# A 3x3 convolution with 2x2 max-pool: ten row sums that read their odd rows from PSUM, casts moved between engines, and a new program order

## The chip, the core and the metric

The kernel runs on one core of a Trainium2 chip. The time is device microseconds of one execution. Five engines matter: TensorE (PE in the profile; its weight loads are PEld), VectorE (DVE), ScalarE (ACT), GpSimd (POOL) and SyncE (SP, which here only issues transfers). Each engine takes its instructions in order and waits on semaphores that other engines and transfers raise.

## The reference

The input x has 16 images of 64 channels and 64x64 pixels, the weights are 128x64x3x3, all float32. The output is the convolution with padding 1, of which the maximum over every 2x2 window is kept: 16 images of 128 channels and 32x32.

```python
for co in range(c_out):
    for ci in range(c_in):
        for kh in range(k):
            for kw in range(k):
                conv[b, co] += weight[co, ci, kh, kw] * x_pad[b, ci, kh:kh+h, kw:kw+w]
...
output[b, c, i, j] = np.max(conv[b, c, i*2:(i+1)*2, j*2:(j+1)*2])
```

## The kernel before

Two images lie side by side in the 128 partitions, 64 channels each (half 0 and half 1). A pair of images is cut into four quarters of 16 rows, so there are 32 steps; a step makes 8 pooled rows of both images. Every product of a step is three matmuls, one per column of the filter, over 64 partitions and up to 512 columns, and lands in one PSUM bank (8 rows of 64). There are eight banks, held in `acc`; a queue `free` gives them out.

The two rows of a pooling window share work: the sum or difference of input rows meets a sum or difference of filter rows. `TYPES` gives each step one of two forms.

- K steps (11 of them) hold x as bf16 (`kx`), loaded with a cast by GpSimd's transfers (`LK`) or cast on chip. PA1 and PA2 build bank `ta`, PB1 and PB2 bank `tb`, and PR adds a product of the row sum `ks` (step KS, a VectorE add).
- W steps (21) hold x as float32 (`wx`, three buffers, loaded by SP: `L`, or `LB`, which also waits for the last VectorE instruction that was marked with `on_vector`). They need three bf16 tiles: `we` (even rows less odd rows, step E), `wd` (each row less the one above, step D, always GpSimd) and `ws` (even rows plus odd rows, step WS, always VectorE). P2 and P0 build `ta`; P3 and P1 build `tb`.

Behind the products: SE copies `ta` to `tb` on ScalarE (W steps, between P2 and P0/P3); EV copies `ta` to SBUF on ScalarE; MX takes the maximum of `tb` and that copy on VectorE, in place; then the shared product (PR or P1) is added; OD copies the odd columns to SBUF on ScalarE; CM takes the maximum of even and odd columns on VectorE; a store follows the second half's CM, on SP. Each of these exists for half 0 and half 1, so `MX.31.1` is step 31, half 1.

`DIFF_ON_VECTOR` names the steps whose E is on VectorE, all others are on GpSimd. `SUM_BY_REDUCTION` names the steps whose WS is a `tensor_reduce` over pairs of rows (one input of 1024 elements) in place of a `tensor_tensor` with two inputs of 512. GpSimd's tensor instructions wait for the last marked VectorE instruction that stands ahead of them in the program (`on_gpsimd`); the `tensor_reduce` isn't marked, the `tensor_tensor` is.

The head: eight matmuls of ones first; the weights arrive as `wraw`, are cast (g0, g1, g2), combined (D0, D2, GS, GM, GP), turned on TensorE (T...), copied out of PSUM (V...). The first K step is cast on chip from `kfirst`, in four pieces (XEa, XEb even rows, XOa, XOb odd rows), the second from `ksecond` (X1, X2). The first K step's products are cut in halves (F.k.part), the first W step's too (G.k.part), with E and D in halves Ea, Eb, Da, Db and the copies SEa, SEb.

The order of everything is written out by hand in `ORDER`, one long list of step names; each engine runs its own steps in that order. Products go through `lanes`: one is issued when a product of the other half stands by, and the six matmuls alternate between the two. Such a couple is called a pair below; there are 132, apart from the halves of F and G.

Of the kernel before, what the change touches and what calls it, by code (L numbers as in the profile page):

```python
# [11 lines left out]
def kernel(  # L12
# [37 lines left out]
    d_pool = ctx.enter_context(tc.tile_pool(name="d_pool", bufs=5))  # L50
    e_pool = ctx.enter_context(tc.tile_pool(name="e_pool", bufs=5))
    ws_pool = ctx.enter_context(tc.tile_pool(name="ws_pool", bufs=5))
    ks_pool = ctx.enter_context(tc.tile_pool(name="ks_pool", bufs=4))
    ev_pool = ctx.enter_context(tc.tile_pool(name="ev_pool", bufs=7))
    od_pool = ctx.enter_context(tc.tile_pool(name="od_pool", bufs=6))
    o_pool = ctx.enter_context(tc.tile_pool(name="o_pool", bufs=6))
# [125 lines left out]

# [85 lines left out]
    def first_product(k, part):  # L268
        s, q = KSTEPS[0], 0
        m0, first, where, skip = (  # L270
            (D2, 1, ta, None),
            (G0, -1, ta, 0),
            (D0, 0, tb, None),
            (G2, 2, tb, None),
        )[k]
        span = (0, R // 2) if part == 0 else (R // 2, R)
        start = k in (0, 2) and part == 0
# [115 lines left out]
    ev, od, ot, made = {}, {}, {}, {}  # L393
# [39 lines left out]
    def colmax(s, h):  # L433
# [5 lines left out]
        made[s] = made.get(s, 0) + 1  # L439
# [10 lines left out]
    def cast_rows(lo, hi):  # L450
        on_vector(nc.vector.tensor_copy(out=kx[0][:, lo:hi:2, :], in_=kfirst[:, lo:hi:2, :]))  # L451

    def cast_more(first):
# [13 lines left out]
        "GM": lambda: on_vector(nc.vector.tensor_sub(out=slots(GM), in0=gsum, in1=g1)),  # L467
        "GP": lambda: on_vector(nc.vector.tensor_add(out=slots(GP), in0=gsum, in1=g1)),
        "XOa": lambda: cast_rows(1, kmid),
        "XOb": lambda: cast_rows(kmid, khi),  # L470
        "XEa": lambda: cast_rows(0, kmid),
        "XEb": lambda: cast_rows(kmid + 1, khi),
# [11 lines left out]
        "SE": seed, "EV": evac, "MX": rowmax, "OD": odd, "CM": colmax,  # L484
    }
# [4 lines left out]
    for m in PRODUCTS:  # L490
# [8 lines left out]
        EV.2.1 P1.3.1 SE.3.1 EV.2.0 WS.3 MX.1.1 P1.1.0 SE.3.0 P0.3.0 MX.2.0 MX.2.1 EV.3.1 PR.2.0 EV.3.0 D.4  # L499
        MX.3.1 OD.2.0 PA1.5.1 OD.1.0 E.4 PA1.5.0 PA2.5.0 P3.3.0 OD.1.1 OD.2.1 L.12 L.14 PA2.5.1 OD.3.1  # L500
        P2.4.1 CM.1.1 CM.2.0 P2.4.0 CM.1.0 PA1.7.1 D.6 EV.5.0 CM.3.1 CM.2.1 MX.3.0 PA2.7.1 PB1.5.1 SE.4.0
        PA1.7.0 PA2.7.0 EV.5.1 SE.4.1 EV.7.0 PB2.5.1 P0.4.1 P0.4.0 P2.6.1 KS.7 E.6 P3.4.1 WS.4 WS.6 P1.3.0
        EV.4.0 PR.5.1 KS.5 WS.8 EV.7.1 P0.6.1 PB1.5.0 PB1.7.0 PB2.5.0 PB2.7.0 L.16 P1.4.1 EV.4.1 MX.5.1
        P3.4.0 OD.3.0 SE.6.1 MX.5.0 LK.1.0 LK.1.1 CM.3.0 MX.4.1 P3.6.1 OD.5.1 PB1.7.1 MX.7.0 PB2.7.1 PR.5.0
        OD.5.0 P2.6.0 EV.6.1 E.8 PR.7.0 MX.4.0 OD.4.1 OD.7.0 CM.5.1 D.8 P1.4.0 SE.6.0 OD.4.0 CM.5.0 E.9
        MX.6.1 CM.7.0 CM.4.0 P1.6.1 P2.8.0 CM.4.1 D.9 P2.8.1 SE.8.0 P0.6.0 P2.9.1 MX.7.1 P3.6.0 OD.6.1
        EV.6.0 P0.8.0 L.17 P3.8.0 SE.8.1 CM.6.1 PR.7.1 EV.8.0 OD.7.1 P0.8.1 MX.6.0 SE.9.1 E.11 MX.8.0 P1.6.0
        D.11 CM.7.1 P2.9.0 OD.6.0 EV.8.1 CM.6.0 WS.9 P3.8.1 P1.8.0 P0.9.1 PA1.10.1 SE.9.0 P2.11.0 OD.8.0
        L.19 L.20 P3.9.1 PA2.10.1 KS.10 EV.9.1 SE.11.0 P0.9.0 CM.8.0 E.14 P2.11.1 MX.9.1 P3.9.0 MX.8.1
        P0.11.0 EV.9.0 EV.10.1 MX.9.0 P1.9.1 D.14 E.12 P1.8.1 PA1.10.0 P3.11.0 PA2.10.0 SE.11.1 OD.9.1  # L510
        P1.9.0 P2.14.0 WS.11 CM.9.1 P0.11.1 P3.11.1 EV.11.0 EV.11.1 OD.8.1 OD.9.0 EV.10.0 P1.11.0 PA1.13.0
        PA1.13.1 MX.11.0 MX.11.1 PA2.13.1 D.12 L.22 L.23 PA2.13.0 P2.12.0 CM.8.1 CM.9.0 D.16 P1.11.1 EV.13.1
        P2.12.1 OD.11.0 SE.14.0 OD.11.1 PB1.10.1 WS.14 P0.14.0 CM.11.0 PB2.10.1 P3.14.0 CM.11.1 L.24 P0.12.0
        SE.12.1 P0.12.1 SE.12.0 P3.12.1 P3.12.0 EV.14.0 PB1.10.0 P2.14.1 WS.12 PB2.10.0 EV.13.0 MX.10.1
        EV.12.1 MX.14.0 E.16 EV.12.0 MX.12.1 PR.10.1 P1.14.0 MX.12.0 SE.14.1 OD.10.1 P1.12.0 PB1.13.1
        PA1.18.0 KS.15 KS.13 CM.10.1 P0.14.1 MX.10.0 OD.14.0 P3.14.1 CM.14.0 EV.14.1 P1.12.1 PR.10.0
        PB2.13.1 WS.16 MX.13.1 PA2.18.0 PA1.15.1 PA2.15.1 PR.13.1 OD.10.0 MX.14.1 PB1.13.0 OD.12.1 EV.18.0
        LK.2.0 P1.14.1 PB2.13.0 P2.16.0 CM.10.0 L.25 PA1.15.0 OD.12.0 EV.15.1 OD.13.1 CM.12.1 PA2.15.0
# [75 lines left out]
```

## Time and profile before

| | |
|---|---|
| median of 3 runs | 104.39 us (104.33 to 104.42) |
| profiled execution, its span | 103.4 us |
| TensorE busy | 96.6 us (93%), 909 matmuls |
| VectorE busy | 91.9 us (89%) |
| ScalarE busy | 82.1 us (79%) |
| GpSimd busy | 75.7 us (73%) |
| mean granted TensorE clock | 0.997 |
| transfers | 23.33 MB, mean 226 GB/s |

The profiled execution has no other time of its own than its span, from the first to the last instruction. Durations overlap on ScalarE and VectorE: the next instruction starts before the one ahead has ended, so that row maxima of 0.69 us start 0.60 us apart. A wait that is put down to one semaphore may have been for several.

### The profile page before, as it was taken

Reading aid. Unit: us, or ns where it says so; the run is one execution under the profiler, and the core shown is the slowest. Engines: PE = TensorE matmul, PEld = TensorE weight load, DVE = VectorE, ACT = ScalarE, POOL = GpSimd, SP = SyncE. Lnnn points to the kernel's source line nnn. Section 1 sums busy time; section 2 is a strip of 40 time slices with the busy share of each in tenths; the row PEclk is TensorE's granted clock in tenths of the full one; section 3 lists DMA queues with packets and bytes.
Section 4 is the critical chain, followed back from the end, with each engine's and each line's share of the span. In section 5 each row is a group of like instructions: output and inputs, shape, how many; then the busy total and the mean of one; then the engine's idle time right before and its main releaser. Section 6 shows DMA issues by size and latency. Waiting matters only on the chain.

```text
span 103.4 us, 2542 instructions
## 1 busy us (share of the span) xinstructions
PE 96.6 (93%) x909; PEld 60.1 (58%) x909; DVE 91.9 (89%) x179; ACT 82.1 (79%) x181; POOL 75.7 (73%) x65
## 2 busy tenths in 40 slices
PE   6889899999999999999999999999999999999910
PEld 2366544555865565577777774556645777776500
DVE  1389899999999999999999999999989996979960
ACT  4545988986789997993887898987899898698820
POOL 6046969773995899998999997959997919970000
PEclk9999999999999999999999999999999999999998
DMA  2989999999899999999847997198699232006252
GB/s 63 265 297 283 389 319 337 384 405 270 219 212 307 304 302 292 341 356 225 175 131 210 252 381 263 51 203 271 173 158 257 80 136 101 0 13 223 74 202 102
DMA packets 13341, 23.33 MB, mean 226 GB/s; under 512 B 1040, under 2 KB 9488, under 8 KB 13328
## 3 DMA queue, kind: packets, MB, share of 16 engines
q1 hardware_dynamic: 12320, 20.68, 61.1%
q0 software_dynamic: 864, 2.36, 13.9%
q8 instruction: 7, 0.11, 0.4%
q10 hardware_dynamic: 144, 0.13, 0.4%
q14 instruction: 6, 0.05, 0.2%
HBM read 17.14 MB, written 8.39 MB: 247 GB/s over the span
## 4 chain that ended last, share of the span: by engine, by line
PE 83%; DMA 6%; DVE 5%; SPq 1%; issue 1%; DVEq 0%
PE acc L200 83%; DMA wx<-in_x_dram 6%; DVE acc L427 2%; DVE o L437 2%; DVE we L353 1%; SPq L114 0%; SPq L113 0%; SPq L109 0%; DVE ks L301 0%; DVEq L589 0%; DVEq L437 0%
## 5 line engine op out<-in xcount | busy, mean ns | idle before, releaser
L200 PEld LDWEIGHTS <-wt 64*128 64x128 bf16 x876 | 57.7, 94 | 34.1 <-issue 1.6
L341 POOL TENSOR_TENSOR wd<-wx 128x1024 bf16<-128x1024 f32 x20 | 47.1, 2360 | 7.6 <-PE acc L200 2.9
L200 PE MATMUL acc<-kx,wt 64*128 64x504 bf16 (+6 forms) x288 | 50.1, 356 | 0.4 <-DVE wt L181 0.4
L200 PE MATMUL acc<-wd,wt 64*128 64x504 bf16 (+3 forms) x264 | 50.1, 367 | 0.0
L427 DVE TENSOR_TENSOR acc<-acc,ev 128x512 f32<-128x512 f32 x64 | 42.0, 693 | 0.9 <-ACT ev L401 0.3
L200 PE MATMUL acc<-we,wt 64*128 64x512 bf16 (+2 forms) x132 | 31.9, 367 | 0.0
L200 PE MATMUL acc<-ws,wt 64*128 64x504 bf16 (+1 forms) x126 | 28.7, 377 | 0.1
L401 ACT ACTIVATE ev<-acc 128x512 f32<-128x512 f32 x42 | 25.1, 608 | 2.7 <-PE acc L200 2.3
L431 ACT COPY od<-acc 128x256 f32<-128x256 f32 x64 | 22.6, 379 | 5.8 <-PE acc L200 5.2
L437 DVE TENSOR_TENSOR o<-acc,od 128x256 f32<-128x256 f32 x64 | 24.5, 416 | 2.1 <-ACT od L431 1.9
L411 ACT COPY acc<-acc 128x512 f32<-128x512 f32 x40 | 23.0, 581 | 3.0 <-PE acc L200 1.7
L332 POOL TENSOR_TENSOR we<-wx 128x512 bf16<-128x512 f32 x16 | 20.2, 1271 | 3.4 <-DVE ws L323 2.4
L200 PE MATMUL acc<-ks,wt 64*128 64x504 bf16 (+1 forms) x66 | 16.5, 377 | 0.4 <-DVE acc L427 0.4
L315 DVE TENSOR_REDUCE ws<-wx 128x512 bf16<-128x1024 f32 x11 | 13.5, 1230 | 0.0
L399 ACT COPY ev<-acc 128x512 f32<-128x512 f32 x22 | 12.9, 595 | 0.6 <-PE acc L200 0.5
L323 DVE TENSOR_TENSOR ws<-wx 128x512 bf16<-128x512 f32 x10 | 7.0, 720 | 0.0
L301 DVE TENSOR_TENSOR ks<-kx 128x512 bf16<-128x512 bf16 x11 | 4.6, 429 | 0.4 <-ACT kx L458 0.4
L551 PE MATMUL acc<-const-bfloat16-1.0 128*128 128x512 bf16 x8 | 3.3, 589 | 0.8 <-PEq L575 0.8
L95 POOL DMA_DIRECT2D kx<-in_x_dram x6 | 3.5, 587 | 0.7 <-DVE kx L451 0.7
L151 POOL COPY wq<-wq 128x64 bf16<-128x64 bf16 x3 | 0.9, 314 | 3.2 <-ACT wq L462 2.5
L465 DVE TENSOR_TENSOR wq<-wraw 128x192 bf16<-128x192 f32 x1 | 0.5, 498 | 2.6 <-DMA wraw<-in_weight_dram 2.6
L368 POOL TENSOR_TENSOR wd<-wx 128x512 bf16<-128x512 f32 x2 | 2.5, 1260 | 0.4 <-DVE we L353 0.4
(30 smaller groups left out, 22.7 us busy)
## 6 DMA issues: line engine op xcount, KB each, us to landing
out_dram<-o SPq DMA_DIRECT2D x31, 256.0 KB, 4.7
wx<-in_x_dram SPq DMA_DIRECT2D x10, 512.0 KB, 7.8
wx<-in_x_dram SPq DMA_DIRECT2D x5, 544.0 KB, 8.7
wx<-in_x_dram SPq DMA_DIRECT2D x5, 480.0 KB, 7.7
kx<-in_x_dram POOLq DMA_DIRECT2D x2, 528.0 KB, 8.5
ksecond<-in_x_dram SPq DMA_DIRECT2D x1, 512.0 KB, 8.0
kx<-in_x_dram POOLq DMA_DIRECT2D x2, 256.0 KB, 6.7
kx<-in_x_dram POOLq DMA_DIRECT2D x1, 496.0 KB, 13.1
```

Of the source, the lines that this page charges most:

```text
L200: nc.tensor.matmul(acc[t][:, i0:i1, o0:o1], wt[lo : lo + CI, tap_of(m0, kw, h), :], rows(lo, i0, i1, c0, c1), start=start and kw == 1, sto ...
L301: nc.vector.tensor_tensor(out=row["ks", s], in0=t[:, f : f + 2 * R : 2, :], in1=t[:, f + 1 : f + 2 * R : 2, :], op=ADD)
L315: nc.vector.tensor_reduce(out=row["ws", s], in_=t[:, f : f + 2 * R, :].rearrange("p (r two) w -> p r w two", two=2), axis=mybir.AxisListTy ...
L323: nc.vector.tensor_tensor(out=row["ws", s], in0=t[:, f : f + 2 * R : 2, :], in1=t[:, f + 1 : f + 2 * R : 2, :], op=ADD)
L332: inst = (nc.vector if vector else nc.gpsimd).tensor_tensor(out=row["we", s], in0=t[:, f : f + 2 * R : 2, :], in1=t[:, f + 1 : f + 2 * R : ...
L341: nc.gpsimd.tensor_tensor(out=row["wd", s], in0=t[:, f + 1 : f + 1 + 2 * R, :], in1=t[:, f - 1 : f - 1 + 2 * R, :], op=SUB)
L399: nc.scalar.copy(out=ev[s, h], in_=acc[t])
L401: nc.scalar.mul(ev[s, h], acc[t], -1.0)
L411: nc.scalar.copy(out=acc[t], in_=acc[ta[s, h]])
L427: nc.vector.tensor_tensor(out=t, in0=t, in1=ev[s, h], op=MAX)
L431: nc.scalar.copy(out=od[s, h], in_=acc[tb[s, h]][:, :, 1::2])
L437: nc.vector.tensor_tensor(out=ot[s][:, h], in0=acc[t][:, :, 0::2], in1=od[s, h], op=MAX)
```

## The change

Ten W steps (4, 6, 8, 12, 16, 17, 19, 22, 23, 28) get a new step XC: ScalarE copies the odd rows from `wx` into a free PSUM bank, and WS adds the even rows from SBUF to that bank. Step 6's E also reads it. Four steps keep the reduction (1, 3, 11, 14); 9 and 20, which had it, become plain sums. E of steps 4 and 11 moves to GpSimd. In the head, XEa, XEb and XOb are cast by ScalarE, g1 by VectorE, GP is made by GpSimd; of the copies out of PSUM, G2 and GM go to VectorE, G1 and GP to ScalarE. Seven pools get more buffers. Stores become steps of their own (ST), placed in the list apart from the CM that they store. `ORDER` is new from beginning to end. The first K step's `tb` is begun by F.3 in place of F.2.

```diff
-    DIFF_ON_VECTOR = (3, 4, 6, 11,)
+    DIFF_ON_VECTOR = (3, 6,)
-    SUM_BY_REDUCTION = (1, 3, 9, 11, 12, 14, 16, 17, 19, 20, 22,)
+    SUM_BY_REDUCTION = (1, 3, 11, 14,)
+    ODD_ROWS_IN_PSUM = (4, 6, 8, 12, 16, 17, 19, 22, 23, 28,)
+    TURNED_BY_SCALAR = ("G0", "G1", "GP",)
+    CAST_BY_SCALAR = ("XEa", "XEb", "XOb",)
+    TAPS_BY_VECTOR = ("g1",)
+    SUMS_BY_GPSIMD = ("GP",)
...
-    d_pool = ctx.enter_context(tc.tile_pool(name="d_pool", bufs=5))
+    d_pool = ctx.enter_context(tc.tile_pool(name="d_pool", bufs=8))
...
-    o_pool = ctx.enter_context(tc.tile_pool(name="o_pool", bufs=6))
+    o_pool = ctx.enter_context(tc.tile_pool(name="o_pool", bufs=8))
...
+    def odd_rows(s):
+        t, f = wx_rows(s)
+        copied[s] = free.popleft()
+        users[s] = 2 if s in DIFF_ON_VECTOR else 1
+        nc.scalar.copy(out=acc[copied[s]], in_=t[:, f + 1 : f + 2 * R : 2, :])
+
+    def with_odd_rows(s, out, op):
+        t, f = wx_rows(s)
+        nc.vector.tensor_tensor(out=out, in0=t[:, f : f + 2 * R : 2, :], in1=acc[copied[s]], op=op)
+        users[s] -= 1
+        if users[s] == 0:
+            free.append(copied[s])
...
+        if s in ODD_ROWS_IN_PSUM:
+            with_odd_rows(s, row["ws", s], ADD)
+            return
...
-        if s == N - 1:
-            store = nc.scalar if made[s] == 1 else nc.sync
-            store.dma_start(out=dst[:, h : h + 1], in_=src[:, h : h + 1])
-        elif made[s] == 2:
+        if h is None:
             nc.sync.dma_start(out=dst, in_=src)
...
     ORDER = """
-        D0 g2 g1 TD0 TG2 g0 D2 XEa LB.3 LB.4 PR.0.1 TD2 VG2 PA1.2.1 VD0 TG0 uG1 TG1 GS F.2.0 VD2 XOa LB.6
-        LB.8 LB.9 GM VG0 F.3.0 XOb F.0.0 uGM F.1.0 VG1 F.0.1 TGM PA2.2.1 XEb LK.0.0 F.1.1 F.2.1 F.3.1 VGM GP
-        Ea KS.0 Eb EV.0.1 G.0.0 EV.0.0 G.0.1 uGP P2.3.1 SEa.0 SEa.1 SEb.1 MX.0.1 Da Db TGP SEb.0 MX.0.0 VGP
-        LK.0.1 X2 PR.0.0 G.1.0 X1 G.2.0 PB1.2.1 PB2.2.1 WS.1 G.2.1 G.1.1 L.11 P0.3.1 PA1.2.0 PA2.2.0 P3.3.1
-        OD.0.0 OD.0.1 EV.1.0 KS.2 E.3 CM.0.1 EV.1.1 P1.1.1 D.3 CM.0.0 PR.2.1 PB1.2.0 P2.3.0 MX.1.0 PB2.2.0
...
+        g0 D2 TD2 g2 TG0 XEa TG2 D0 XOb VG0 XEb GS XOa VD2 LK.0.0 VG2 GM TD0 uGM VD0 F.0.0 F.3.0 g1 F.0.1 F.2.0
+        GP F.3.1 uG1 LB.3 TGM KS.0 F.1.1 F.1.0 uGP EV.0.1 EV.0.0 Ea TG1 VG1 F.2.1 VGM LB.4 Eb G.0.0 MX.0.1 TGP
+        G.0.1 SEa.1 Da LB.6 Db MX.0.0 PR.0.0 SEb.1 LK.0.1 WS.1 SEa.0 PR.0.1 SEb.0 X2 OD.0.1 X1 PA1.2.1 G.2.0
+        OD.0.0 G.1.0 G.1.1 CM.0.1 PA2.2.1 G.2.1 EV.1.1 PA1.2.0 PA2.2.0 VGP E.3 EV.1.0 CM.0.0 P2.3.0 KS.2 D.3
+        MX.1.1 PB1.2.0 P2.3.1 MX.1.0 PB2.2.0 EV.2.0 EV.2.1 WS.3 SE.3.1 P1.1.1 OD.1.1 PB1.2.1 P1.1.0 PB2.2.1 E.4
...
+        CM.26.1 P0.30.0 EV.29.0 P2.31.0 P1.28.1 OD.28.0 CM.28.0 OD.28.1 ST.25 CM.28.1 PB1.29.0 SE.30.1 PB1.29.1
+        PB2.29.0 PB2.29.1 P0.30.1 P2.31.1 P3.30.1 KS.29 EV.30.0 SE.31.0 EV.30.1 P0.31.0 SE.31.1 P3.31.0 MX.29.1
+        P0.31.1 ST.21 WS.31 EV.31.0 P3.30.0 P3.31.1 ST.28 MX.29.0 ST.26 PR.29.0 MX.30.1 MX.31.0 EV.31.1 PR.29.1
+        OD.29.0 MX.30.0 P1.30.1 P1.31.0 OD.29.1 MX.31.1 OD.31.0 CM.29.0 P1.30.0 P1.31.1 ST.20 CM.29.1 CM.31.0
+        OD.30.1 ST.29 OD.30.0 CM.30.1 OD.31.1 CM.30.0 ST.31.0 ST.30 CM.31.1 ST.31.1
```

More of the change, by code (lines that the diff above doesn't have):

```diff
@@ L276, in first_product @@
         span = (0, R // 2) if part == 0 else (R // 2, R)
-        start = k in (0, 2) and part == 0
+        start = k in (0, 3) and part == 0
         if start:
@@ L331, in we @@
         vector = s in DIFF_ON_VECTOR
+        if vector and s in ODD_ROWS_IN_PSUM:
+            with_odd_rows(s, row["we", s], SUB)
+            return
         inst = (nc.vector if vector else nc.gpsimd).tensor_tensor(
@@ L438, in colmax, with store @@
         free.append(t)
-        made[s] = made.get(s, 0) + 1
+    def store(s, h=None):
         p, q = place[s]
@@ L466 @@
         "GS": lambda: on_gpsimd(nc.gpsimd.tensor_tensor(out=gsum, in0=g0, in1=g2, op=ADD)),
[L467 to L472, printed above, removed]
+        "GM": lambda: tap_sum("GM", GM, SUB),
+        "GP": lambda: tap_sum("GP", GP, ADD),
+        "XOa": lambda: cast_rows("XOa", 1, kmid),
+        "XOb": lambda: cast_rows("XOb", kmid, khi),
+        "XEa": lambda: cast_rows("XEa", 0, kmid),
+        "XEb": lambda: cast_rows("XEb", kmid + 1, khi),
         "X1": lambda: cast_more(0),
@@ L484 @@
         "SE": seed, "EV": evac, "MX": rowmax, "OD": odd, "CM": colmax,
+        "XC": odd_rows, "ST": store,
     }
@@ L499 @@
[L499 to L518, printed above, removed]
```

119 lines of the change are left out of this document (76 added, 43 removed).

## The prediction

> **What bounds the kernel now.** I read the page's busy shares and its chain of waits first.
>
> ```profile
> PE 96.6 (93%) x909; PEld 60.1 (58%) x909; DVE 91.9 (89%) x179; ACT 82.1 (79%) x181; POOL 75.7 (73%) x65
> ...
> PE 83%; DMA 6%; DVE 5%; SPq 1%; issue 1%; DVEq 0%
> ```
>
> TensorE is the end-setting engine; the 6% DMA are the first loads, the 5% DVE mostly the end. The stretches by 10 us show whether it ever stands still between:
>
> ```profile
> 10.00:20.00 10.00, 9.57 (x105) 5.11 (x102) 9.40 (x17) 8.80 (x21) 8.25 (x6) 1.00 1.05 353
> ...
> 30.00:40.00 10.00, 10.00 (x97) 5.61 (x93) 9.98 (x19) 9.39 (x21) 8.50 (x5) 1.00 1.02 298
> 40.00:50.00 10.00, 10.00 (x96) 6.57 (x94) 10.00 (x18) 7.63 (x18) 9.49 (x7) 1.00 0.99 288
> ```
>
> The columns are PE, PEld, DVE, ACT, POOL, granted clock, DMA share, GB/s. TensorE is full from 15 us to the end while DVE is at 100% too, and DVE's saturation costs TensorE nothing. The work there is pairs of products, six matmuls that start 0.648 us apart (pair starts 92.25, 92.90, 93.55). From the first pair at 13.02 to the last but one at 96.79 there are 129 steps, 83.59 us at that pitch; 83.77 are used. So the middle loses 0.2 us in all. Time can change only before 13 us, at the end, or by new stalls.
>
> The head, and the end, by the timeline (start, length, engine, operation):
>
> ```profile
> 9.81 2.49 POOL L368 TENSOR_TENSOR wd<-wx 128x512 bf16<-128x512 f32 x2 [0.37 <-DVE we L353]
> ...
> 13.02 1.67 PE L200 MATMUL acc<-kx,wt 64*128 64x512 bf16 x13
> ...
> 97.73 2.07 DVE L437 TENSOR_TENSOR o<-acc,od 128x256 f32<-128x256 f32 x6
> ```
>
> Head: step 1's rows land at 8.57 and 9.13 us, Ea/Eb read them, Da/Db run behind them on GpSimd until 12.30, the last halves of G need Db, and the pairs begin at 13.02. End: six column maxima stand back to back behind the row maxima, then the last store (issue 99.83, the trace's end 103.4).
>
> **The sums.** By the rows of groups:
>
> ```profile
> L427 DVE TENSOR_TENSOR acc<-acc,ev 128x512 f32<-128x512 f32 x64 | 42.0, 693 | 0.9 <-ACT ev L401 0.3
> ...
> L411 ACT COPY acc<-acc 128x512 f32<-128x512 f32 x40 | 23.0, 581 | 3.0 <-PE acc L200 1.7
> ...
> L315 DVE TENSOR_REDUCE ws<-wx 128x512 bf16<-128x1024 f32 x11 | 13.5, 1230 | 0.0
> ```
>
> DVE: five reductions (12, 16, 17, 19, 22) become a sum with one PSUM operand. No row has that with an SBUF result; between 683 ns (both operands SBUF, line 332) and 720 (plain row sum, line 323), nearest is line 427 at 693, which also reads PSUM and SBUF. 5 x (1230-693) = 2.7 us. Two reductions (9, 20) become plain sums, 2 x 510 ns = 1.0; differences 4 and 11 go to GpSimd, 1.4; sums 4, 6, 8, 23, 28 and difference 6 change by 0.1 together. DVE -5.2 us, worth nothing to TensorE beyond the 0.2 and the end. ACT: ten SBUF-to-PSUM copies, between 581 (line 411, PSUM to PSUM) and 630 ns (line 458, from SBUF), taken near line 411 as 0.59: +5.9 us. Its idle before PE-released work (5.2 us in 12 waits of the odd-column copy) covers that on average; if not, see the third rival. GpSimd: two differences of 1.27, and GP at 0.8: +3.3 on 75.7, it runs a step ahead. TensorE: the same products plus one zeroing matmul (about 0.2) in the gap before PR.0 at 10.99, where it idles 0.43 now. Buffers: with eight output tiles and late stores, a tile is taken again after its store at the earliest some 5 us after SP can issue it (SP runs ahead of the program's positions), and stores land in a median 4.7: nothing, and about 2 us on DVE for any one that misses. SP's order: loads that now stand behind a store that waits for its maximum are L.14 (ST.5, near 28 us), L.20 (ST.7, 33) and L.25 (ST.15, 60); GpSimd reads them near 41, 52 and 75, loads land in 7.8 us: nothing. GpSimd's LK.1.0 goes out near 24 instead of 21.56; with the longest landing, 13.1, it is there at 37.1, and PA1.10 comes at 37.7: nothing.
>
> **Head replayed.** DVE D2, D0, XOa at 5.48 (kfirst lands 5.46), then VD2 to 6.13, VG2 to 6.43, GM, VD0 to 7.15, g1 to 7.4; ACT casts XEa 5.48, XOb 6.28 (lands 6.26), VG0 to 7.17, XEb to 7.5, each cast 0.45 between 0.36 (line 423, 256 wide) and 0.63 (line 458). F.0.0 starts at 6.19 (F's first half now: 6.22) and F ends near 9.4 (9.42). Ea at 8.59, VGM behind it, Eb to 9.66 (now 9.73), Db to 12.23, PA1.2 at 13.0. The EV.0, MX.0, SE steps fall within 0.1 us of where they are. So casts on other engines give 0.0, bounds -0.1 to +0.1: the same rows and Db rule.
>
> **Where it gives way.** POOL's bf16 load LK.0.0 now waits for XEb's cast and goes out at 8.28; behind XOa it goes out at about 6.1. SP's LB.3 waited for XEa (out at 5.86); it now waits for g1 (7.45), with LB.4 behind Ea (9.05), LB.6 behind Eb (9.7), LB.8 behind KS.2. Issues in four stretches (queue 1 is SP's, queue 0 GpSimd's; "us to landing" last):
>
> ```profile
> wx<-in_x_dram SPq DMA_DIRECT2D x1, 544.0 KB, 6.8
> ...
> kx<-in_x_dram POOLq DMA_DIRECT2D x1, 256.0 KB, 8.3
> ...
> q1 hardware_dynamic: 148, 0.55, 102.6%
> ...
> q1 hardware_dynamic: 115, 0.40, 52.7%
> q0 software_dynamic: 97, 0.20, 52.1%
> ```
>
> LB.3 (first line) landed at 12.63, LK.0.0 at 16.54. The third line is 11.0 to 12.3 us, before LK.0.0 moves: 114 packets/us. The last two are 12.6 to 14.6: SP's queue falls to 57/us. LK.0.0 has 144 packets, 3.0 us, so it costs the loads beside it 1.5 us. So far LB.4 and LB.6 paid. Its first packet came 4.0 us after issue, other loads' of that queue (21.56, 46.51, 74.31) 1.5 to 1.8 after. From 6.1 that is 7.7 to 10.1, before LB.3 lands in either case. So LB.3 lands between 12.63 (the traffic falls into time that queue 1 leaves idle because LB.3 comes later) and 14.1. I take 13.7: LB.6 and LB.8, which shared with that queue, landed 2.09 and 2.47 us after the load ahead, the next two 1.33 and 1.20, some 1.1 each.
>
> The Trainium skill ("DMA: Bandwidth & Descriptors", section on queues, rings and completion order) says that each DMA engine takes turns between queues, packet by packet. The halving agrees (114 to 57 packets/us); by the rule alone LB.3 would pay all 1.5 us and the sum would be 105.5.
>
> What waits: E.3 on DVE needs LB.3. In order behind it stand CM.0.0, KS.2, MX.1.1, starts 0.60, 0.33 and 0.34 apart (pitches of back-to-back rows), and MX takes 0.69: P1.1.1, in the fourth pair, can start 2.02 us after LB.3. Its place is 13.0 + 3 x 0.648 = 14.95, so LB.3 may land at 12.93; at 13.7 TensorE stands 0.8 us. D.3, behind KS.2, asks 13.1 of it for P0.3. The full middle gives nothing back. Lower end 0, upper 1.2.
>
> **End.** P3.30.0 and P3.31.1 share a pair three before the last, two row maxima follow (end + 0.6 + 0.69), and again six column maxima stand behind. The last maximum starts at 96.93 to 97.17 (now 97.12), the latter because P0.31.1 comes two pairs after P2.31.1 with a 0.57 copy between. Taken -0.1, bounds -0.2 to +0.05.
>
> **Sum.** The profiled execution's own time is its span, 103.4; the three runs' median is 104.39, 1.0 around it, taken as unchanged. 103.4 + 0.8 - 0.1 = 104.1 in span, 104.39 + 0.7 = 105.1 as a time. Own range of this case 104.6 to 105.6.
>
> **Rivals.**
> First, LK.0.0 hits step 1's rows instead: with 1.6 us to first packet (7.7) it takes turns with what lands at 8.57 and 9.13. Eb, Da, Db shift by up to 1.2 us and PA1.2 with them; LB.3's delay is then inside that, not added. 105.3 to 105.6. For it: 1.5 to 1.8 at three issues; against: 4.0 in just this stretch. I count it into the forecast's case, 0.44 together.
> Second, the other side: a freer DVE. If LB.3 lands by 12.93, the head costs nothing and DVE's 5.2 us lift the 0.2 us of stalls and up to 0.2 at the end: 104.0, 103.8 if the head's 0.1 comes too. It decides at that landing. For it: LB.4 to LB.9 no longer run beside step 1's rows; or LK.0.0 starts past 12.6, 6.5 us after issue, where 4.0 is the longest seen (0.05 of the chance). Chance 0.26 in all. The Trainium skill ("SBUF — State Buffer", section "SBUF: two separate sides") says that DVE copies using both ports keep GpSimd from writing its load's descriptors; by that rule LK.0.0 starts late here too. Its 4.0 us would agree, but nothing shown tells the lock from other causes.
> Third, ACT becomes the bound: by stretches of 13 pairs (8.43 us) its steps at row pitches (0.49, 0.48, 0.27, copies 0.5) ask 8.0 of the busiest against 7.2 where they come now. A seed copy has three pairs, 1.94, less 0.81, 0.58 and 0.07 of handover: 0.48 slack. A copy of 0.5 in front uses it; if four of ten end 0.25 late, +1.0: 105.3. Chance 0.13.
> Fourth, all cancels: late by 0.2 or not at all and no gain, 104.2 to 104.6. Chance 0.17. Also here: the PSUM operand saves nothing (sums stay at 1230), as DVE is not the bound.
>
> **Numbers.** 0.2% (0.21 us) is about what a measurement of this kernel can tell. Slower: 0.44 + 0.13 = 0.57; same 0.17; faster 0.26. The range goes from the second rival's 103.8 to 105.8, the first's 105.6 with the end's spread.
>
> **What would show it.** The sums near 693 and copies near 590 ns; E.3 idle until LB.3 lands past 13 us and a TensorE wait near 15; pitch 0.648 after that. E.3 starting by 12.9 makes the forecast wrong; a middle with TensorE waiting on seed copies makes the third rival right.

## The result, and the profile after

| | before | changed |
|---|---|---|
| time, median, on one chip | 104.62 us (104.33 to 105.20) | 105.90 us (105.64 to 106.33) |
| ratio | | 1.0121 (1.0087 to 1.0156) |
| profiled execution, its span | 103.4 us | 104.3 us |
| the time of that execution | not timed | 106.1 us |

The change makes the kernel 1.2% slower. The forecast had the sign (slower, with a chance of 0.57) but fell 0.8 us short: 105.1, with a range that ended at 105.8, 0.1 below the measured time. Busy shares and the chain of work that ended last in the changed kernel, from its page:

```profile
PE 98.0 (94%) x910; PEld 59.4 (57%) x910; DVE 89.2 (86%) x174; ACT 87.1 (83%) x193; POOL 78.8 (76%) x68
...
PE 79%; DMA 10%; DVE 6%; issue 1%; SPq 0%; DVEq 0%
```

VectorE lost 2.7 us net, ScalarE gained 5.0, and TensorE still sets the end. The share of DMA in the chain grew from 6 to 10%. Stretches of 10 us, with the columns that the prediction names:

```profile
10.00:20.00 10.00, 9.47 (x95) 5.00 (x95) 8.55 (x15) 8.54 (x21) 6.91 (x6) 1.00 0.97 276
...
30.00:40.00 10.00, 10.00 (x97) 7.32 (x94) 9.62 (x19) 9.44 (x22) 9.69 (x7) 1.00 0.97 279
40.00:50.00 10.00, 10.00 (x96) 7.16 (x93) 9.70 (x21) 9.54 (x22) 9.11 (x7) 1.00 0.65 176
```

From 20 us on TensorE is full, as before. Between 10 and 20 us it issued 95 matmuls where it had issued 105: the loss is there. From pair 14 (22.45 us; before 21.48) to the last pair the two traces take the same, 76.06 and 75.96 us; behind the last pair the changed kernel needs 5.80 in place of 5.95. So 0.97 us are lost ahead of pair 14. The timeline of that part (start, length, engine, operation, and in brackets the idle time before it and what ended it, the releaser):

```profile
4.57 0.81 POOL L509 TENSOR_TENSOR gsum<-wraw 128x192 f32<-128x192 f32 x1 [2.31 <-DVE wq L508]
...
4.77 0.77 DVE L494 CAST kx<-kfirst 128x256 bf16<-128x256 f32 x1 [0.28 <-DMA kfirst<-in_x_dram]
...
5.93 1.91 PE L219 MATMUL acc<-kx,wt 64*128 64x256 bf16 x30 [0.24 <-DVE wt L188]
...
7.50 0.72 POOL L198 TENSOR_TENSOR wq<-gsum,wraw 128x192 bf16<-128x192 f32 x1 [0.58 <-DVE wq L192]
7.60 0.91 DVE L393 TENSOR_TENSOR we<-wx 128x256 bf16<-128x256 f32 x1
...
10.62 1.41 ACT L463 COPY acc<-acc 128x256 f32<-128x256 f32 x4 [0.33 <-ACT wt L184]
...
12.09 1.49 PE L219 MATMUL acc<-wd,wt 64*128 64x256 bf16 x24 [0.30 <-ACT acc L463]
...
13.41 1.47 PE L219 MATMUL acc<-kx,wt 64*128 64x512 bf16 x12
...
13.84 0.69 DVE L372 TENSOR_TENSOR we<-wx 128x512 bf16<-128x512 f32 x1 [0.54 <-DMA wx<-in_x_dram]
```

The same instructions of before (the cast XOa, Ea, and the four copies SEa and SEb):

```profile
6.41 0.48 DVE L451 CAST kx<-kfirst 128x256 bf16<-128x256 f32 x1
...
8.59 0.42 DVE L353 TENSOR_TENSOR we<-wx 128x256 bf16<-128x256 f32 x1 [0.21 <-DMA wx<-in_x_dram]
...
10.35 1.30 ACT L423 COPY acc<-acc 128x256 f32<-128x256 f32 x4 [0.47 <-ACT ev L399]
```

Three things are to be seen. The cast XOa takes 0.77 us and Ea 0.91, where the same forms took 0.28 to 0.48 and 0.42 to 0.46 before; each stands while GpSimd runs a filter sum (GS, then GP). Before's XOa, at 0.48, met GS too. In the nine profiles of this case in which GS holds XOa up, XOa ends 0.15 us behind GS, whenever it began; in the others it takes 0.28 to 0.30. In ten profiles Ea ends 0.28 us behind GP in the same way. The first pair starts at 13.41 instead of 13.02, behind the copies SEa and SEb on ScalarE (the releaser at 12.09), which end at 12.04 where they ended at 11.64. And E.3 waits for step 3's rows until 13.84; behind it P1.1.1, P0.3 and PR.2.0 cost TensorE 0.30, 0.09 and 0.19 us beyond the pitch (0.648 us from pair to pair) at 16.3, 17.7 and 18.5. The 0.39 us of the first pair and these 0.58 make the 0.97.

### The profile page after: what moved, and what is told of

It is laid out like the page before. It is cut to its first block, busy times and chain, and to the rows that moved or that the text cites. A ratio compares the mean times of both kernels' runs of the same rounds, so it can differ in the third digit from the quotient of the medians.

```text
span 104.3 us, 2548 instructions
## 1 busy us (share of the span) xinstructions
PE 98.0 (94%) x910; PEld 59.4 (57%) x910; DVE 89.2 (86%) x174; ACT 87.1 (83%) x193; POOL 78.8 (76%) x68
## 4 chain that ended last, share of the span: by engine, by line
PE 79%; DMA 10%; DVE 6%; issue 1%; SPq 0%; DVEq 0%
PE acc L219 79%; DMA wx<-in_x_dram 6%; DMA kfirst<-in_x_dram 3%; DVE o L477 2%; DVE acc L467 1%; DVE wt L188 1%; DVE kx L494 1%; DVE wq L200 0%; DVE wq L192 0%; SPq L115 0%; DVE ks L320 0%; DVEq L633 0%; DVE we L372 0%; DVEq L467 0%
## 5 line engine op out<-in xcount | busy, mean ns | idle before, releaser
L219 PEld LDWEIGHTS <-wt 64*128 64x128 bf16 x876 | 56.5, 94 | 35.7 <-issue 3.0
L219 PE MATMUL acc<-wd,wt 64*128 64x504 bf16 (+3 forms) x264 | 52.5, 367 | 0.3 <-ACT acc L463 0.3
L467 DVE TENSOR_TENSOR acc<-acc,ev 128x512 f32<-128x512 f32 x64 | 43.0, 692 | 2.6 <-PE acc L219 1.0
L219 PE MATMUL acc<-we,wt 64*128 64x512 bf16 (+3 forms) x132 | 31.0, 367 | 0.0
L477 DVE TENSOR_TENSOR o<-acc,od 128x256 f32<-128x256 f32 x64 | 25.5, 417 | 4.7 <-ACT od L471 3.4
L372 POOL TENSOR_TENSOR we<-wx 128x512 bf16<-128x512 f32 x18 | 22.8, 1277 | 1.2 <-PE acc L219 0.9
L339 DVE TENSOR_TENSOR ws<-wx,acc 128x512 bf16<-128x512 f32 x10 | 6.7, 677 | 0.1
L335 ACT COPY acc<-wx 128x512 f32<-128x512 f32 x10 | 6.1, 609 | 0.0
L360 DVE TENSOR_TENSOR ws<-wx 128x512 bf16<-128x512 f32 x7 | 5.0, 709 | 0.0
L352 DVE TENSOR_REDUCE ws<-wx 128x512 bf16<-128x1024 f32 x4 | 4.9, 1226 | 0.0
```

What stands on the lines that cost most here:

```text
L219: nc.tensor.matmul(acc[t][:, i0:i1, o0:o1], wt[lo : lo + CI, tap_of(m0, kw, h), :], rows(lo, i0, i1, c0, c1), start=start and kw == 1, sto ...
L335: nc.scalar.copy(out=acc[copied[s]], in_=t[:, f + 1 : f + 2 * R : 2, :])
L339: nc.vector.tensor_tensor(out=out, in0=t[:, f : f + 2 * R : 2, :], in1=acc[copied[s]], op=op)
L372: inst = (nc.vector if vector else nc.gpsimd).tensor_tensor(out=row["we", s], in0=t[:, f : f + 2 * R : 2, :], in1=t[:, f + 1 : f + 2 * R : ...
L467: nc.vector.tensor_tensor(out=t, in0=t, in1=ev[s, h], op=MAX)
L477: nc.vector.tensor_tensor(out=ot[s][:, h], in0=acc[t][:, :, 0::2], in1=od[s, h], op=MAX)
```

## The experiments

A gap "over before" is the ratio less one, times before's median of the same runs; the changed kernel's is 1.2 to 1.3 us. A TensorE wait is the start of a pair less that of the pair ahead, less 0.648. Times inside a kernel come from one profiled execution each, and executions of one kernel differ by 1 us and more, so the times over all executions decide what a change is worth.

**Step 3's rows: an early issue, a late GpSimd load, a shorter turn.** Against a repeat of the changed kernel on the same chip:

```diff
@@ e1 @@
-... GS XOa VD2 LK.0.0 ... uG1 LB.3 TGM ... VGM LB.4 Eb ...
+... GS XOa LB.3 LB.4 VD2 LK.0.0 ... uG1 TGM ... VGM Eb ...
@@ e2 @@
-... VD2 LK.0.0 VG2 ... TGM KS.0 F.1.1 ...
+... VD2 VG2 ... TGM KS.0 LK.0.0 F.1.1 ...
@@ e3 @@
-... MX.0.1 TGP G.0.1 SEa.1 ...
+... MX.0.1 G.0.1 TGP SEa.1 ...
```

> The changed kernel as it is, on the chip on which the three edits beside it run. All theories: slower than the kernel before by 0.9 to 1.3 us; the span 103.9 to 104.6. If the difference of the times is larger than that of the spans, part of the loss lies outside the traced span.

> Only LB.3 and LB.4 move in the list, to right behind XOa, so that they go out near 5.9 us in place of 7.38 and 9.05. Theory A (step 3's rows land at 13.81 because their load is issued late, after which SP's queue stands idle from 8 to 9.5 us): they land by 12.9, E.3 starts by 13.0, the TensorE waits near 15.9 and 17.7 us go, and the kernel gains 0.4 to 0.6 us on the changed one. Theory B (they land late because GpSimd's early bf16 load takes turns with them): they then share the engines with it from 7.5 on, land past 13.4, and under 0.2 us is gained. Theory C (traffic ahead of step 1's rows is what hurts): step 1's rows land later than 6.97 and 7.67 on the same clock and the kernel is slower still.

> Only GpSimd's load LK.0.0 moves, from behind XOa to behind KS.0, so that it goes out near 8.6 us in place of 5.85; LB.3 stays where it is. Theory B: LB.3 lands by 12.9 and 0.4 to 0.6 us is gained on the changed kernel. Theory A: nothing is gained, and something is lost if the load's packets, some 1.6 to 4 us after issue, now fall on LB.3's: it lands at 13.8 to 15, and the kernel is 0 to 1 us slower than the changed one.

> Only TGP, three transposes on TensorE, moves from ahead of G.0.1 to behind it. Theory D (the head's first 0.4 us is TGP in front of G.0.1, behind which the four seed copies and then G.2.0 wait): SEa.1 starts at about 10.4 in place of 10.62, G.2.0 at about 11.85 in place of 12.09, PA1.2 at 13.15 to 13.2 in place of 13.41. The wait for step 3's rows stays, so in the time this is worth 0 to 0.25 us: 0 if that wait takes all of it up, as theory A says of a load that lands at 13.8 whatever TensorE does. Rival: VG1 ahead of the seed copies on ScalarE is what holds them; then they start at 10.62 as now.

Measured: e0 106.13 us, 1.0117 (1.008 to 1.0154); e1 105.78, 1.0080 (1.0053 to 1.0107); e2 105.94, 1.0086 (1.0054 to 1.0117); e3 106.31, 1.0128 (1.0092 to 1.0164). In e1 LB.3 is issued at 5.54 and lands at 12.3, the waits before 20 us are gone, and by the medians 0.35 us come back, though the intervals of e0 and e1 overlap. In e2 LB.3 is issued at 7.38, as in the changed kernel, but lands at 12.0 instead of 13.8. Queue 1 is SP's, queue 0 GpSimd's; from 8 to 9.5 us in the changed kernel:

```profile
q0 software_dynamic: 98, 0.18, 76.5%
q1 hardware_dynamic: 10, 0.03, 7.6%
```

and in e2, where GpSimd's load comes later:

```profile
q1 hardware_dynamic: 78, 0.32, 71.2%
```

So LK.0.0 does hold up step 3's rows, by 1.8 us at equal issue. The order of issue goes with which load waits: in the seven profiles in which LK.0.0 goes out ahead of LB.3, its first packet comes 1.4 to 1.9 us after issue and LB.3 takes 6.0 to 7.0 us to land (4.6 in e2); in the thirteen in which it goes out behind LB.3, its first packet comes after 2.6 to 5.0. Moving it doesn't pay in full: e2 shows two new TensorE waits of 0.27 us, at 22.16 and 25.67, at PA1.7.0 and P3.4.0. In e3 the turn TGP no longer stands between G.0.0 and G.0.1, and the way from the first half product to the first pair falls from 7.48 to 7.11 us; E.3 then waits all the longer, and nothing is won. Part of that longer wait is this execution's own, the slowest of e3's six (106.84): its rows land 0.8 us later than in the changed kernel's. E.3 in e3's timeline:

```profile
14.62 0.69 DVE L372 TENSOR_TENSOR we<-wx 128x512 bf16<-128x512 f32 x1 [1.50 <-DMA wx<-in_x_dram]
```

and among e3's waits from 13 to 20 us (in total, times, longest), the one that TensorE has for E.3:

```profile
PE acc L219 <- DVE we L372: 0.7, 1, 0.7
```

The head's delay and step 3's rows can thus hide one another; the next runs take both away.

The repeat e0 shows how much an execution decides. Its profile is the fastest of its six (105.33):

```profile
4.56 0.29 DVE L494 CAST kx<-kfirst 128x256 bf16<-128x256 f32 x1
...
13.08 0.69 DVE L372 TENSOR_TENSOR we<-wx 128x512 bf16<-128x512 f32 x1
```

XOa starts just ahead of GS (4.62) and isn't held, and step 3's rows land at 13.06 and cost TensorE 0.13 us in place of 0.58. The first pair stands at 13.10 all the same, though F.0.0 starts 0.66 us earlier than in the changed kernel's first profile (5.27).

**Both, then GpSimd's filter sum too.**

e5 is e1 and e3 together; e9 changes e5 by this:

```diff
-... XEb GS XOa LB.3 LB.4 VD2 LK.0.0 VG2 GM TD0 uGM VD0 ...
+... XEb XOa LB.3 LB.4 GS VD2 LK.0.0 VG2 TD0 VD0 GM uGM ...
```

> The changed kernel with both moves of the two runs before it: LB.3 and LB.4 right behind XOa, and TGP behind G.0.1. Theory head (the whole loss is made before the tenth pair: step 3's rows cost 0.3 us, TGP ahead of G.0.1 another 0.3, and alone the second was taken up by step 3's rows): the two add, PA1.2 stands 7.1 us behind F.0.0, no TensorE wait before 20 us, 0.5 us below the changed kernel, about 105.5 us. Rival (whatever is gained ahead of 20 us is given back by the middle, whose order has no room): no better than the early load alone, 105.8.

> The kernel with the early load and TGP behind G.0.1, and in addition GS (GpSimd's filter sum) behind the cast XOa instead of ahead of it, and VD0 ahead of GM. Theory lock (an instruction of VectorE with SBUF operands that meets a running GpSimd sum stands until that is through: XOa took 0.77 us beside GS, 0.29 without): XOa takes 0.29 to 0.36 us, F.0.0 starts 0.8 us behind the landing of kfirst's first half where the changed kernel needs 1.18, and the time falls from 105.4 to 105.0 to 105.3. Rival (F waits for something else, such as VD2 or XOb, and the cast has room): XOa short, but F.0.0 no nearer to the landing, 105.4.

Measured: e5 105.42, 1.0061 (1.0029 to 1.0092); e9 105.20, 1.0049 (1.0023 to 1.0075). In e9:

```profile
4.60 0.28 DVE L494 CAST kx<-kfirst 128x256 bf16<-128x256 f32 x1
...
4.97 0.82 POOL L509 TENSOR_TENSOR gsum<-wraw 128x192 f32<-128x192 f32 x1 [2.70 <-DVE kx L494]
```

XOa takes 0.28 us and the first pair stands at 12.67, with no TensorE wait before 50 us. But F.0.0 starts 1.18 us behind the landing of kfirst's first half (4.44), no nearer than in the changed kernel, since VD2 now waits for the turn of D2 instead: on that point the rival was right. Of 1.2 us, 0.6 came back with e5; the further step to e9 is within the intervals, and that it comes from the shorter cast is not shown.

**Which half of the kernel carries the loss.** e6 has before's head up to PA2.2.0 and the changed rest, e7 the changed head up to D.3 and before's rest with before's sums and differences, no XC, and each store directly behind its second CM; each head with its own engines for casts, turns and filter sums:

```diff
@@ e6 @@
-        g0 D2 TD2 g2 TG0 XEa TG2 D0 XOb VG0 XEb GS XOa VD2 LK.0.0 ...
+        D0 g2 g1 TD0 TG2 g0 D2 XEa LB.3 LB.4 PR.0.1 TD2 VG2 ... TG0 uG1 TG1 GS F.2.0 ... PA1.2.0 PA2.2.0 ...
@@ e7 @@
-        ... P2.3.0 KS.2 D.3 MX.1.1 PB1.2.0 P2.3.1 MX.1.0 PB2.2.0 EV.2.0 ...
+        ... P2.3.0 KS.2 D.3 LB.8 LB.9 P2.3.1 PB1.2.1 PB2.2.1 L.11 P0.3.1 P3.3.1 P1.1.1 ...
```

> The program order of before up to PA2.2.0, with its engines for casts, turns and sums of the filter, and the changed kernel's order, sums and stores behind that. Theory head: the loss is gone, 105.0 us as before (104.8 to 105.1 if the end's 0.15 us shows). Rival (the middle and the end cost as much as the head: TensorE waits of 0.1 to 0.2 us near 56, 76, 78 and 96 us): 105.4 to 105.6, with those waits in the trace.

> The changed kernel's head up to D.3 with its engines, and behind it the order of before with its sums and differences, each store directly behind its second column maximum. Theory head: as slow as the changed kernel, 105.9 to 106.2. Rival (middle and end): half or less of the loss, 105.0 to 105.5.

Measured: e6 105.50, 1.0047 (1.0015 to 1.0079); e7 106.65, 1.0147 (1.0092 to 1.0202). Neither simple theory holds. The changed head alone is as slow as the whole change (in its trace TensorE waits 0.67 us more for D.3, which stands behind CM.0.0 and KS.2 in that head, while before's order asks for it in the sixth pair; so that wait belongs to the seam of the two orders, and e7 does not measure the head by itself). But before's head doesn't bring all back: 0.5 us stay, and the trace of e6 has waits of 0.17, 0.08 and 0.20 us at 15.7, 17.1 and 17.9. There VectorE stands like this:

```profile
13.21 0.68 DVE L372 TENSOR_TENSOR we<-wx 128x512 bf16<-128x512 f32 x1
13.81 0.42 DVE L477 TENSOR_TENSOR o<-acc,od 128x256 f32<-128x256 f32 x1
14.15 0.42 DVE L320 TENSOR_TENSOR ks<-kx 128x512 bf16<-128x512 bf16 x1
14.48 1.29 DVE L467 TENSOR_TENSOR acc<-acc,ev 128x512 f32<-128x512 f32 x2
```

E.3 no longer waits for its rows; it stands behind CM.0.1, and CM.0.0 and KS.2 stand between it and MX.1.1, for which P1.1.1 waits, fourth pair in the changed order. Before had P1.1.1 in the eighth pair, beside PR.2.0.

**The chain at step 3 taken apart.**

```diff
@@ e14, from e6 @@
-... OD.0.0 CM.0.1 EV.1.1 E.3 EV.1.0 CM.0.0 P2.3.0 KS.2 D.3 MX.1.1 PB1.2.0 ... P0.3.1 CM.1.1 D.4 MX.2.0 ...
+... OD.0.0 KS.2 E.3 D.3 CM.0.1 EV.1.1 MX.1.1 EV.1.0 CM.0.0 P2.3.0 PB1.2.0 ... P0.3.1 MX.2.0 CM.1.1 D.4 ...
```

> Before's head with the changed kernel's rest, and in it KS.2 and E.3 ahead of CM.0.1 on VectorE, MX.1.1 directly behind that, D.3 behind E.3, and MX.2.0 ahead of CM.1.1. With before's head alone TensorE still waited 0.17, 0.08 and 0.20 us near 15.7, 17.1 and 17.9 us. Theory chain (the changed order puts P1.1.1 fourth behind a chain of five VectorE instructions, and these waits are what is left of the loss): no wait before 50 us, 104.7 to 105.1, 0.45 below that kernel. Rival (what is left is spread over the rest): 105.3 to 105.5 as before.

Measured: 104.88, 1.0006 (0.9975 to 1.0038). MX.1.1 now starts 0.93 us behind E.3 instead of 1.27, and D.3 ends 3.13 behind it instead of 3.79:

```profile
13.00 0.68 DVE L372 TENSOR_TENSOR we<-wx 128x512 bf16<-128x512 f32 x1
13.60 0.42 DVE L477 TENSOR_TENSOR o<-acc,od 128x256 f32<-128x256 f32 x1
13.93 0.69 DVE L467 TENSOR_TENSOR acc<-acc,ev 128x512 f32<-128x512 f32 x1
```

Of the three waits one of 0.10 is left, and with it goes all that could be measured. So the loss is located: the changed head (with its order of loads), and the changed order's first pairs behind it. The sums from PSUM, the stores apart and the rest of the order together neither cost nor bring more than this interval's 0.4 us.

**Before's head once more.**

> The kernel before once more, for a second profile. In the first one step 1's rows landed at 8.57 and 9.13 us, and the first pair stood at 13.02. Theory head (before's head is shorter than that profile shows, since the rows were late): with rows that land before 8 us the first pair stands at 12.2 to 12.8 us, 6.4 to 6.8 behind the first half product, and the span is 102.5 to 103.0. Rival (the head is bounded by its own chain, the copies SE and E and D, and not by the rows): first pair at 12.9 or more whatever lands when.

Measured, one execution: 104.68 us, span 102.9. Theory head (before's head is shorter when the rows come early) holds in it:

```profile
12.47 0.83 PE L200 MATMUL acc<-kx,wt 64*128 64x512 bf16 x6
12.50 0.68 DVE L332 TENSOR_TENSOR we<-wx 128x512 bf16<-128x512 f32 x1
```

The first pair stands at 12.47, 6.63 behind the first half product, and not at 13.02: Ea starts at 7.92 without a wait for step 1's rows, where it waited for them until 8.59 in the first profile. Before's spans in the runs go from 102.4 to 104.2, with a mean of 103.1; the first profile's 103.4 was one of the longer ones. Over the six profiles with before's head (before, e6, e14, e15, e17, e18) the first pair stands at 12.47 to 13.02, on average 12.84; over the eight with the changed kernel's head steps in their order, loads apart (changed, e0, e1, e2, e7, e8, e10, e19), at 12.91 to 13.65, on average 13.34. That is 0.5 us for the head.

**The sums.**

Both leave the XC steps out of the changed kernel.

```diff
@@ e8 @@
-    ODD_ROWS_IN_PSUM = (4, 6, 8, 12, 16, 17, 19, 22, 23, 28,)
-    SUM_BY_REDUCTION = (1, 3, 11, 14,)
+    ODD_ROWS_IN_PSUM = ()
+    SUM_BY_REDUCTION = (1, 3, 9, 11, 12, 14, 16, 17, 19, 20, 22,)
@@ e10 @@
-    ODD_ROWS_IN_PSUM = (4, 6, 8, 12, 16, 17, 19, 22, 23, 28,)
-    SUM_BY_REDUCTION = (1, 3, 11, 14,)
+    ODD_ROWS_IN_PSUM = ()
+    SUM_BY_REDUCTION = (1, 3, 4, 6, 8, 11, 12, 14, 16, 17, 19, 22, 23, 28,)
```

> The changed kernel without its XC steps: eleven sums by reduction as before, the others plain, all else in place. It takes 5.9 us from ScalarE and gives VectorE back some 2.7 us. Theory sums for nothing (TensorE is full, VectorE's share is cover): 106.0 to 106.3, as the changed kernel. Rival one (the order needs the short sums: VectorE late at its maxima, and TensorE waits for P1 of the steps with a reduction): over 106.6. Rival two (the copies delay ScalarE's seed and evacuation copies, so taking them out helps): 105.7 or less.

> The changed kernel without XC steps, all ten sums as reductions (1230 ns, one SBUF operand) in place of sums that read PSUM (677 ns); nothing else. Without the PSUM sums, but with plain sums in five of their places, the time was 113.1, and those sums took up to 2.73 us beside GpSimd. Theory lock (those plain sums stood behind GpSimd, and that made the 7 us): reductions stand at 1230 ns beside GpSimd, VectorE has 5.5 us more in all, and its 10% of room take most of it: 106.1 to 107.5. Rival length (VectorE is at its limit in this order, any 5 us more on it come out at the end): 109 to 113.

Measured: e8 113.11, 1.0786 (1.0738 to 1.0834); e10 109.77, 1.0471 (1.0437 to 1.0504). The row sums by group, of the changed kernel (PSUM operand, then two SBUF operands), of e8 and of e10:

```profile
L339 DVE TENSOR_TENSOR ws<-wx,acc 128x512 bf16<-128x512 f32 x10 | 6.7, 677 | 0.1
L335 ACT COPY acc<-wx 128x512 f32<-128x512 f32 x10 | 6.1, 609 | 0.0
...
L360 DVE TENSOR_TENSOR ws<-wx 128x512 bf16<-128x512 f32 x7 | 5.0, 709 | 0.0
```

```profile
L360 DVE TENSOR_TENSOR ws<-wx 128x512 bf16<-128x512 f32 x10 | 12.9, 1296 | 0.0
```

```profile
L352 DVE TENSOR_REDUCE ws<-wx 128x512 bf16<-128x1024 f32 x14 | 17.1, 1229 | 0.0
```

In e8 the plain sum, 709 ns in the changed kernel, takes 1296. WS.6 and WS.4 in its timeline, VectorE and then GpSimd:

```profile
22.80 3.33 DVE L360 TENSOR_TENSOR ws<-wx 128x512 bf16<-128x512 f32 x2
```

```profile
22.63 2.35 POOL L381 TENSOR_TENSOR wd<-wx 128x1024 bf16<-128x1024 f32 x1 [1.66 <-DVE we L372]
```

WS.6 was issued 0.17 us behind GpSimd's D.6 and ended at 25.53, 0.55 behind that one's end: it stood for the whole of it, and took 2.73 us. Reductions (one SBUF operand), sums with a PSUM operand and maxima, of which dozens overlap GpSimd in every trace, keep their length. The rival, length, has the greater part: e10 has no stretched sum, VectorE has 5.5 us more to do (10 x (1229 - 677) ns), and the gap over before grows by 3.7. That is above theory lock's 106.1 to 107.5 and inside the 109 to 113 of rival length. The standing behind GpSimd has its part too: e8 has three reductions fewer than e10, plain sums in their place, and is still 3.3 us slower. So the changed order needs its short sums; before's order had put eleven reductions where TensorE didn't wait for them.

**Attempts at a faster kernel.** e12 and e13 have a head written anew (LB.3, LB.4, GS behind XOa; g1 cast by ScalarE; GP and three turns' copies on VectorE; the halves of F together, TG1 and TGP behind G.0.1) ahead of the changed rest (P1.1.1 one pair later) and of before's. e16 is e9 with g1 cast by ScalarE, TG1 ahead of F.0.0 and VG1 right behind F.3.0. e15 is e14 with PR.29.1 ahead of P0.31.1; e18 is e15, and e19 the changed kernel, with ten output tiles:

```diff
@@ e12, e13 @@
-... F.3.1 ... TGM ... F.1.0 ... TG1 VG1 F.2.1 VGM ... TGP G.0.1 SEa.1 ...
+... F.0.1 F.2.0 F.1.0 F.1.1 TGM F.3.1 F.2.1 ... G.0.0 MX.0.1 G.0.1 TG1 TGP VG1 MX.0.0 VGP SEa.1 ...
@@ e16 @@
-... TG0 XEa ... TD0 VD0 ... F.0.0 F.3.0 g1 ... TG1 VG1 F.2.1 ...
+... TG0 g1 XEa ... TD0 TG1 VD0 ... F.0.0 F.3.0 VG1 ... F.2.1 ...
@@ e15 @@
-... P0.31.1 ... EV.31.1 PR.29.1 ...
+... PR.29.1 P0.31.1 ... EV.31.1 ...
@@ e18, e19 @@
-    o_pool = ctx.enter_context(tc.tile_pool(name="o_pool", bufs=8))
+    o_pool = ctx.enter_context(tc.tile_pool(name="o_pool", bufs=10))
```

> The changed kernel with a head of its own: LB.3, LB.4 and GS behind XOa, g1 cast by ScalarE between XEa and XOb, GP made by VectorE, G1, GP, GM turned out by VectorE, the halves of F without turns but TGM between, TG1 and TGP behind G.0.1, P1.1.1 one pair later. Theory head (nothing but the head stands between the changed kernel and a lower time): PA1.2 6.5 to 7.0 us behind F.0.0, no wait before 20 us, 104.2 to 104.8, below before's 104.9. Rival (the transfers, busy 97% and over from 10 to 40 us, then set the pace of the steps, and waits for E and D appear between 17 and 50 us): 105.0 or more.

> The same new head, with LB.6 to LB.9 behind Ea, ahead of the order, sums and differences of before (no XC steps). Theory head: 104.2 to 104.8, as with the changed kernel's rest, and so the ten sums and the new order bring nothing by themselves. Rival (the order of before is fixed to its own head: its E.3, D.3 and P0.3 chain makes new waits near 17 us): 105.0 or more.

> The changed kernel with the early load, TGP behind G.0.1 and GS behind XOa (105.2 us), and now TG1 ahead of F.0.0 instead of among the halves of F, with g1 cast by ScalarE ahead of XEa and VG1 out ahead of the copies EV.0. Theory turns (each turn among the halves of F and G costs its 0.27 to 0.34 us, since TensorE is full from F.0.0 to G.0.1): PA1.2 6.7 to 6.8 us behind F.0.0, where it was 7.05, and 104.9 to 105.1, what is left over before being gone. Rival (the turn ahead of F.0.0 delays F itself by as much): no difference, 105.2.

> The same, with PR.29.1 moved ahead of P0.31.1, which waited 0.20 us for the copy SE.31.1 at the end. Theory: that wait goes, the column maxima at the end don't move up by all of it: 0.1 to 0.2 below the kernel without it, 104.5 to 105.0, and so as fast as before or faster. Rival (the end is set by VectorE's ten last instructions and not by TensorE): no difference.

> The kernel with before's head, the short chain at step 3 and PR.29.1 ahead (105.10 us, 104.49 to 106.44), with ten output tiles in place of eight. In its profile CM.15.1 stood 1.3 us for the store of step 12, whose tile it takes, and TensorE 0.8 us at 58.6. Theory tiles (a store that now and then lands over 8 us after its issue costs up to 0.8 us in some executions): that wait is gone, the times lie between 104.4 and 105.3, median 104.6, at or below before. Rival (the spread is that of the first loads): median and spread stay at 105.0 and 104.5 to 106.4.

> The changed kernel with ten output tiles in place of eight, nothing else. Theory tiles: 105.8 to 106.0, 0.1 to 0.3 below the changed kernel, since few of its executions lose there. Rival: 106.1.

Measured: e12 106.42, 1.0161 (1.0123 to 1.0200); e13 105.37, 1.0062 (1.0037 to 1.0086); e16 105.46, 1.0065 (1.0033 to 1.0097); e15 105.10, 1.0023 (0.9993 to 1.0054); e18 105.00, 1.0010 (0.9985 to 1.0036); e19 105.89, 1.0083 (1.0052 to 1.0114). None beats before. The new head fails by its own order: VG1 stands between MX.0.1 and MX.0.0 and waits for TG1, so PR.0 starts at 11.78 in e12 (10.97 in the changed kernel) and the pairs with it; part of that is this execution's late landing of step 1's rows, at 8.28. In e16 TG1 is out of the way and the first pair is still 7.06 us behind F.0.0, since F.0.1 and the maxima come later; that each turn among the halves costs its own length is not shown. In e15 the wait at the end is gone, and the time is no better; in its profile VectorE waits for a store's tile instead:

```profile
57.64 0.42 DVE L477 TENSOR_TENSOR o<-acc,od 128x256 f32<-128x256 f32 x1 [1.32 <-DMA out_dram<-o]
```

CM.15.1 waits for the store of step 12, and TensorE 0.80 us at 58.6. That stall is in two of the profiles with the changed rest and eight tiles (0.55 us in e5). With ten tiles the wait is gone in both kernels; the gaps of 0.1 (e18 against 0.2) and 0.9 (e19 against 1.2) lean that way and lie within the intervals. e19's profile has two other TensorE waits, of 0.34 and 0.23 us at 65.7 and 71.2, which weren't followed up. So it stays open whether the wait for a store's tile has a part in the loss.

## Why the prediction was right or wrong

**Head replayed, "0.0": wrong, and this term made most of the miss.** The step that failed is "casts on other engines give 0.0, bounds -0.1 to +0.1: the same rows and Db rule". Measured at the first pair: +0.39 between the two first profiles, +0.94 against before's second profile (12.47), 0.5 on average over the profiles. Three parts of the replay failed. XOa was taken at its length alone, and took 0.77 us beside GS; Ea likewise 0.91 beside GP. "The EV.0, MX.0, SE steps fall within 0.1 us of where they are" left out that TG1 now stands ahead of F.2.1 and TGP ahead of G.0.1 (0.34 us each on TensorE), so SEb ended 0.40 later although F began 0.29 earlier. And "the same rows and Db rule" held for an execution with late rows; with earlier rows the copies SE rule, as at 12.09 here. How the head's loss divides between the two turns, the held instructions and the loads is open: e3 shows 0.37 us for TGP inside one trace, e0 shows the delay without a held XOa, and no time tells the parts apart. The Trainium skill ("SBUF — State Buffer", section "SBUF: two separate sides") states that VectorE, when it reads two SBUF inputs or uses both ports, and a GpSimd instruction exclude each other for a whole instruction, the first one going first. WS.6's 2.73 us agree, and so do XOa and Ea, which end a fixed 0.15 and 0.28 us behind GpSimd's sum. The prediction had used that section for GpSimd's load and not for these.

**The sum: its starting point was wrong.** It added "1.0 around it, taken as unchanged". In each of the runs since, before and changed alike, the time is 1.71 to 1.85 us over the span. So the span of 103.4 belongs to a time of some 105.2: the profiled execution lay 0.8 above the median of 104.39, and the text read the difference as work around the span. The +0.7 was thus found in a slow execution, in which late rows hid the head's loss, and added to the median of faster ones, where the change costs 1.28. The other 0.2 of the miss is before's own median, 104.62 over six runs where three had given 104.39. Against before's second profile (span 102.9) the account closes: 0.94 at the first pair, 0.58 behind it, 0.09 from pair 14 on and -0.17 at the end make the 1.4 us by which the spans differ. That the forecast span of 104.1 came so near to the changed kernel's 104.3 is luck: between the first two profiles 0.39 for 0.0 in the head and 0.58 for 0.8 at step 3 nearly cancel.

**Where it gives way: right in its cause.** E.3 started at 13.84 for 13.7, P1.1.1 started 2.02 us behind it as reckoned, and the cause holds: LK.0.0 costs LB.3 1.8 us at equal issue, where 1.1 were taken and 1.5 were the rule's. TensorE stood 0.58 us for the 0.8 forecast, since the first pair was itself late by 0.39; in e0's execution it stood 0.13. The chain E.3, CM.0.0, KS.2, MX.1.1 is the one that e14 took apart. That it costs without late rows as well (e6) was not foreseen.

**The sums: right in size, too simple in worth.** 677 ns for 693, copies 609 for 590, and nothing won. The sums and differences took VectorE's forecast 5.2 us off by their rows; its busy time fell by 2.7 alone, since the maxima, as long as before, overlap less (rows of 42.0 and 24.5 us now fill 43.0 and 25.5) and KS, Ea and Eb ran longer. But it is not that they save nothing: without them the changed order loses 3.7 us. The middle is full in both kernels, each with its own way to keep VectorE off TensorE's path.

**Buffers, "nothing":** one output tile was missed, 0.5 us on VectorE in the changed kernel's profile, nothing on TensorE there.

**End, -0.1:** -0.15 behind the last pair, and P0.31.1 cost 0.20 ahead of it, as the text named.

**Rivals.** The first didn't come: step 1's rows landed at 6.63 and 7.33, ahead of LK.0.0's first packets near 7.5. The second needed the rows at 12.93; e2 had them at 12.0 and was still slower by 0.9, so early rows alone did not bring it. The third didn't: the stretch from pair 14 on, which holds eight of ScalarE's ten copies, is 0.10 us longer in the one profile of each. The fourth, that all cancels, is what before's head and e14's chain show for the rest of the change. The 0.2% that the prediction holds a measurement can tell was too small: before's executions alone have spans from 102.4 to 104.2.

## What to carry to other kernels

One profiled execution is one draw: before adding to its span, compare it with a time of the same execution, and ask which landing in it was late and what it hides. In a head, where GpSimd and VectorE change tasks, look up for each VectorE instruction with two SBUF operands or an SBUF cast which GpSimd instruction runs beside it; if the GpSimd one started first, the VectorE one stands for about that one's rest, not for a share of it. Two delays of one path can hide each other, so an experiment that removes one may show nothing.

## What the runs showed of the hardware

- A VectorE sum of two SBUF operands took 0.68 us alone and up to 2.73 behind a GpSimd difference already running; a reduction (1.23 us), a sum with one PSUM operand (0.677) and a maximum on PSUM (0.69) didn't change.
- While 98 packets of GpSimd's load moved, SP's queue moved 10 where it moves 78 without them. The Trainium skill ("DMA: Bandwidth & Descriptors", section on queues, rings and completion order) has the engines take turns packet by packet; the halving in the profile before fitted that, this doesn't. Here the load issued first went ahead and the other hardly moved; why is open.
- XOa ended 0.15 us behind GpSimd's GS in all nine profiles in which GS held it, and Ea 0.28 us behind GP in all ten, however late within the sum they had begun.
- ScalarE's copy from SBUF to PSUM took 609 ns, from PSUM to PSUM 590 in the same profile.
